# Loading the weights of a batched matmul two matrices at a time in 12 KB runs, with the x cast on ScalarE and products in 32-column tiles

## The chip, the cores and the metric

One core of a Trainium2 chip. The metric is device time in microseconds (us) of the whole program; the runs of one version lie within 0.05 to 0.26% of each other here (0.47% for one). Every kernel is compared with the kernel before on the same chip. Ratios are the mean time of one kernel's fast runs over that of the other's of the same rounds, so they aren't quite the ratio of the medians quoted beside them. The runs were made on several chips; the kernel before took 523.76 to 524.06 us in their rounds, so medians of different rounds compare to some 0.3 us. The 95% interval of a ratio is about 0.9 us wide to each side.

The engines in the profile are PE (TensorE; PEld is its weight load), DVE (VectorE), ACT (ScalarE), POOL (GpSimd) and SP (SyncE, which issues all transfers here). Data moves on 16 DMA engines. In this kernel every transfer has 128 rows and is moved as 128 packets, and for every 8 of them there is a 4-byte packet that reports completion: the kernel before has 24,832 of the first and 3,104 of the second.

## The reference

```python
b1, b2, m, k, n = 8, 16, 256, 512, 384
x      = randn(b1, b2, m, k)   # float32
weight = randn(b1, b2, k, n)   # float32
return np.matmul(x, weight).astype(np.float32)
```

128 independent products of 256 x 512 by 512 x 384: 67 MB of x and 101 MB of weights are read, 50 MB are written.

## The kernel before

It works in groups of four batches (the last four are cut into two pairs). A group's x is one transfer, each row of a batch matrix of weights is its own run, and the output is one transfer. Casts to bf16 are on VectorE, transposes of x and products on TensorE, and ScalarE copies the products out of PSUM.

```python
def load(e, a):                     # SyncE
    ...                             # x: 128 rows, 16 KB each, one transfer a group
    for i in range(G):              # weights: one matrix a transfer, 128 rows of 6 KB
        e.wait_ge(w_cast, a.m + (i + 1 - WS))
        e.dma_start(w_sb[...][:],
            w_rows[...].rearrange("(p ko) n -> p ko n", ko=KO)).then_inc(...)

def cast(e, a):                     # VectorE
    e.tensor_copy(out=x_bf[...], in_=x_sb[...]).then_inc(x_cast, 1)   # 128 x 4096
    cast_w(0)                                                         # 128 x 1536
    for q in range(G):                                                # transposes out of PSUM
        e.tensor_copy(out=xt[...], in_=pt[...]...).then_inc(t_copied, 1)
    for i in range(1, G):
        cast_w(i)

def copy_out(e, a):                 # ScalarE: 16 copies a group, 32 rows each
    for i in range(G):
        for g in range(G):
            e.copy(out=out_sb[...][i * C : (i + 1) * C, g : J * G : G, :],
                   in_=po[...][g * C : (g + 1) * C, :, :N])
```

SyncE issues the loads three groups ahead of the stores, all on one queue: first the loads of group n + 3, then the store of group n. A load waits until its buffer's last content has been cast.

## Time and profile before

| | kernel before |
|---|---|
| time | 524.05 us (first three runs), 523.94 with a fourth |
| span of the profiled run | 521.7 us |
| DMA | 218.16 MB in 27,940 packets, 9 tenths busy or more in 38 of 40 slices |
| busy share of PE, DVE, ACT | 62%, 52%, 78% |

A row of the slices cuts the span into 40 equal parts, and each digit is the busy share in tenths. Since the DMA row is full from end to end and no compute row is, the table is read as: the transfers set the time. The prediction below shows the lines.

### The profile page before, as it was taken

What the parts mean: (1) busy time and instruction counts of PE and PEld (TensorE: products, weight loads), DVE (VectorE), ACT (ScalarE), POOL (GpSimd) and SP (SyncE); (2) the same over time, 40 slices, a digit from 0 to 9 for tenths busy, and PEclk for the clock granted to TensorE, in tenths of its full rate; (3) what the DMA queues carried; (4) which work ended last, traced back from release to release, by engine and by line L of the source; (5) the groups of instructions that cost most, each with busy time, mean ns of one, the idle gap of its engine ahead of it and who ended that gap; (6) DMA issues with size and microseconds to landing.
All of it is one profiled execution on the core that took longest, in us unless ns stands there. A gap on an engine that the chain in (4) does not pass through costs nothing.

```text
span 521.7 us, 5583 instructions
## 1 busy us (share of the span) xinstructions
PE 323.8 (62%) x1536; PEld 192.3 (37%) x1536; DVE 270.0 (52%) x289; ACT 406.9 (78%) x511; POOL 0.7 (0%) x6
## 2 busy tenths in 40 slices
PE   1666565675767666675666856667566656666563
PEld 1433233442434333443334433243333434333341
DVE  2666546644466444566345663446644466444551
ACT  0699997697796879778977699777898786886972
POOL 0000000000000000000000000000000000000000
PEclk9999989667696687769677596787967896677976
DMA  8999999999999999999999999999999999999996
GB/s 330 424 422 423 421 427 423 424 423 423 426 431 424 422 421 426 428 429 421 420 427 427 428 424 421 423 427 429 427 422 421 425 429 428 422 423 423 426 427 258
DMA packets 27940, 218.16 MB, mean 418 GB/s; under 512 B 3104, under 2 KB 3104, under 8 KB 19744
## 3 DMA queue, kind: packets, MB, share of 16 engines
q1 hardware_dynamic: 27936, 218.12, 99.8%
q8 instruction: 1, 0.02, 0.0%
q14 instruction: 3, 0.02, 0.0%
HBM read 167.77 MB, written 50.33 MB: 418 GB/s over the span
## 4 chain that ended last, share of the span: by engine, by line
DMA 89%; DVE 7%; issue 1%; PE 1%; SPq 0%; DVEq 0%; ACTq 0%; ACT 0%
DMA x_sb<-in_x_dram 85%; DVE x_bf L158 7%; DMA w_sb<-in_weight_dram 4%; PE po L197 1%; SPq L121 0%; DVE x_t L167 0%; DVE w_bf L152 0%; DVEq L157 0%; ACTq _compat.py:109 0%; ACT out_sb L213 0%; SPq L304 0%; SPq L49 0%
## 5 line engine op out<-in xcount | busy, mean ns | idle before, releaser
L213 ACT COPY out_sb<-po 32x768 f32<-32x768 f32 (+1 forms) x504 | 397.9, 790 | 107.4 <-PE po L197 100.6
L197 PE MATMUL po<-w_bf,x_t 128*128 128x384 bf16 x1024 | 227.6, 380 | 139.9 <-ACT out_sb L213 103.6
L197 PEld LDWEIGHTS po<-w_bf,x_t 128*128 128x128 bf16 x1024 | 104.2, 109 | 254.7 <-ACT out_sb L213 126.9
L158 DVE CAST x_bf<-x_sb 128x4096 bf16<-128x4096 f32 (+1 forms) x33 | 73.6, 2229 | 215.6 <-DMA x_sb<-in_x_dram 215.6
L184 PE MATMUL pt<-identity,x_bf 128*128 128x128 f32 x512 | 96.9, 365 | 50.6 <-DVE x_bf L158 50.6
L152 DVE CAST w_bf<-w_sb 128x1536 bf16<-128x1536 f32 x128 | 117.5, 952 | 1.7 <-DMA w_sb<-in_weight_dram 1.5
L184 PEld LDWEIGHTS pt<-identity,x_bf 128*128 128x128 f32 x512 | 88.1, 218 | 67.0 <-issue 62.3
L167 DVE COPY x_t<-pt 128x1024 bf16<-128x1024 bf16 x128 | 84.4, 687 | 22.9 <-PE pt L184 22.3
L213 ACT ACT_TABLE_LOAD x7 | 9.0, 1283 | 1.6 <-ACTq L277 1.5
masks.py:199 POOL TENSOR_SCALAR_AFFINE_SELECT identity<-identity 128x128 f32<-128x128 f32 x1 | 0.3, 292 | 0.2 <-POOL identity L238 0.2
L238 POOL MEMSET identity<- 128x128 f32 x1 | 0.2, 204 | 0.5 <-SPq L49 0.5
L293 POOL MEMSET const-bfloat16-1.0<- 128x1 bf16 x1 | 0.1, 101 | 0.0
L293 POOL MEMSET const-uint8-127<- 128x1 uint8 x1 | 0.1, 101 | 0.0
L293 POOL MEMSET const-float32-0.0<- 128x1 f32 x1 | 0.1, 98 | 0.2 <-issue 0.2
L293 POOL MEMSET const-float32-1.0<- 128x1 f32 x1 | 0.1, 98 | 0.0
## 6 DMA issues: line engine op xcount, KB each, us to landing
w_sb<-in_weight_dram SPq DMA_DIRECT2D x128, 768.0 KB, 28.0
x_sb<-in_x_dram SPq DMA_DIRECT2D x31, 2048.0 KB, 29.6
out_dram<-out_sb SPq DMA_DIRECT2D x31, 1536.0 KB, 27.4
x_sb<-in_x_dram SPq DMA_DIRECT2D x2, 1024.0 KB, 24.3
out_dram<-out_sb SPq DMA_DIRECT2D x2, 768.0 KB, 8.4
```

The lines of the kernel that those rows point to most:

```text
L152: e.tensor_copy(out=w_bf[(a.m0 + i) % WBS][:], in_=w_sb[(a.m0 + i) % WS][:]).then_inc(w_cast, 1)
L158: e.tensor_copy(out=x_bf[a.slot(BS)][:, : J * G], in_=x_sb[a.slot(XS)][:, : J * G]).then_inc(x_cast, 1)
L167: e.tensor_copy(out=xt[:, j, :, :, g : g + 2].rearrange("k h i g c e -> k g (h i) (c e)"), in_=pt[(a.m0 + q) % PT][:].bitcast(bf16).rearrange(
L184: ins = e.transpose(pt[(a.m0 + q) % PT][:, rr, h, :], words[:, 2 * q + rr, h :: KO // 2], identity[:],)
L197: ins = e.matmul(po[(a.m0 + i) % PO][:, j, :N], xt[:, j, ko // 2, i, :, :, ko % 2].rearrange("k g c -> k (g c)"), w_bf[(a.m0 + i) % WBS][: ...
L213: ins = e.copy(out=out_sb[a.slot(OS)][i * C : (i + 1) * C, g : J * G : G, :], in_=po[(a.m0 + i) % PO][g * C : (g + 1) * C, :, :N],)
L238: e.memset(identity[:], 0.0).then_inc(id_done, 1)
L293: nc = _bacc.Bacc("TRN2", target_bir_lowering=False, num_devices=1)
```

## The change

The intent is fewer and longer contiguous runs in the weight loads. A row of two matrices is 12 KB only if a row holds eight consecutive rows of weights; the first matrix then lies in lanes 0 to 63, the second in 64 to 127, and each cast takes a half of the lanes to the half where it belongs. The contraction index is thereby permuted, so x must be permuted alike, which its cast does, now on ScalarE. And the products of the four batches share one PSUM tile, 32 rows each, so that one copy of 128 rows takes them out. Loads run four groups ahead, the last four batches are no longer cut into pairs, and the last group's store goes out in four pieces.

```diff
-            e.dma_start(
-                w_sb[(a.m0 + i) % WS][:],
-                w_rows[bass.ds(a.m * K + i * K, K)].rearrange("(p ko) n -> p ko n", ko=KO),
+        for d in range(G // D):                      # D = 2 matrices a load
+            e.dma_start(
+                w_sb[slot][:],
+                w_rows[bass.ds(n * (G * K) + d * (D * K), D * K)].rearrange(
+                    "(p k) n -> p k n", k=S * KO     # 8 rows, 12 KB
 ...
+            for a in range(D):                       # VectorE: half-lane casts
+                for h in range(S):
+                    e.tensor_copy(
+                        out=w_bf[...][h * HP : (h + 1) * HP],
+                        in_=w_sb[slot][a * HP : (a + 1) * HP, h * KO : (h + 1) * KO, :],
+                    ).then_inc(w_cast, 1)
 ...
-        e.tensor_copy(out=x_bf[...], in_=x_sb[...]).then_inc(x_cast, 1)
+        for h in range(S):                           # ScalarE, after two output copies
+            ins = e.copy(out=x_bf[...][:, :, h],
+                in_=x_sb[...].rearrange("p r (q s c) -> p r s q c", s=S, c=KO)[:, :, h])
 ...
+                    for i in range(G):               # TensorE: four tiles of 32 columns
+                        mine = slice(i * C, (i + 1) * C)
+                        ins = e.matmul(po[...][mine, rr, :N],
+                            x_t[...][:, 2 * q + rr, ko // 2, mine, ko % 2], w_bf[...][:, ko, :], ...)
 ...
-    LAG = 3
+    LAG = 4
```

## The prediction

> **What bounds the kernel now.** I read the page's slices first, then its DMA parts, the chain of work that ended last, the costliest groups, and last the timeline of one steady group and of the tail.
>
> ```profile
> ACT  0699997697796879778977699777898786886972
> DMA  8999999999999999999999999999999999999996
> GB/s 330 424 422 423 421 427 423 424 423 423 426 431 424 422 421 426 428 429 421 420 427 427 428 424 421 423 427 429 427 422 421 425 429 428 422 423 423 426 427 258
> DMA packets 27940, 218.16 MB, mean 418 GB/s; under 512 B 3104, under 2 KB 3104, under 8 KB 19744
> ...
> DMA 89%; DVE 7%; issue 1%; PE 1%; SPq 0%; DVEq 0%; ACTq 0%; ACT 0%
> ```
>
> The DMA row is at 9 in 38 of 40 slices and the rate is flat at 420 to 431 GB/s; only the first and the last slice are low. The chain is 89% DMA. So the kernel moves 218 MB through 16 full engines, and no compute engine sets its time. The ACT row is the highest compute row, but it has gaps everywhere, and the groups say what they are:
>
> ```profile
> L213 ACT COPY out_sb<-po 32x768 f32<-32x768 f32 (+1 forms) x504 | 397.9, 790 | 107.4 <-PE po L197 100.6
> ...
> L158 DVE CAST x_bf<-x_sb 128x4096 bf16<-128x4096 f32 (+1 forms) x33 | 73.6, 2229 | 215.6 <-DMA x_sb<-in_x_dram 215.6
> ...
> L152 DVE CAST w_bf<-w_sb 128x1536 bf16<-128x1536 f32 x128 | 117.5, 952 | 1.7 <-DMA w_sb<-in_weight_dram 1.5
> ...
> L167 DVE COPY x_t<-pt 128x1024 bf16<-128x1024 bf16 x128 | 84.4, 687 | 22.9 <-PE pt L184 22.3
> ```
>
> VectorE, the first consumer, waits 215.6 us for x. A steady group of four batches takes 16.13 us: the x casts of the timeline start at 255.99, 272.14 and 288.28.
>
> ```profile
> 255.99 2.29 DVE L158 CAST x_bf<-x_sb 128x4096 bf16<-128x4096 f32 x1 [7.70 <-DMA x_sb<-in_x_dram]
> 258.41 3.33 PE L184 MATMUL pt<-identity,x_bf 128*128 128x128 f32 x16 [1.88 <-DVE x_bf L158]
> 262.81 2.76 PE L197 MATMUL po<-w_bf,x_t 128*128 128x384 bf16 x16 [1.07 <-DVE x_t L167]
> 270.78 2.74 PE L197 MATMUL po<-w_bf,x_t 128*128 128x384 bf16 x8 [0.91 <-ACT out_sb L213]
> 272.14 2.29 DVE L158 CAST x_bf<-x_sb 128x4096 bf16<-128x4096 f32 x1 [6.97 <-DMA x_sb<-in_x_dram]
> ```
>
> The two product bursts give the pace of a 384-column matmul: less the 0.33 us of the last one's own duration, (2.76 - 0.33) / 15 = 162 ns with the clock free, and (2.74 - 0.49) / 7 = 321 ns with it halved.
>
> **What a packet costs** decides the gain, and the page doesn't show it, so I sorted the trace's packet records by size. There is one packet per contiguous run (16,640 of 6,144 B, 3,968 of 12,288 B, 3,968 of 16,384 B), so runs aren't cut. Shortest durations: 234, 460 and 611 ns, so 4,096 B more cost 151 ns (434 GB/s over 16 engines) and the rest is about 7 ns a packet whatever its size. Packets overlap a little, so durations overstate; I fitted 2 us windows between 50 and 480 us (16 engines times the window = sum of packets times cost) and got 235 ns for 6 KB, 458 for 12 KB and 609 for 16 KB. Check: a group has per engine 8 x 16 KB, 32 x 6 KB and 8 x 12 KB packets: 4.87 + 7.52 + 3.66 = 16.05 us, against 16.13 measured. Idle engine time, counted from the same records, is 0.3 us in all up to 507 us, and 2.8 us (averaged over 16 engines) after it: the tail.
>
> [...]
>
> **The change, part by part.**
>
> *Weight loads.* 16,384 packets of 6 KB become 8,192 of 12 KB: 8,192 x (2 x 235 - 458) / 16 = 6.1 us less of full DMA time. If reads of 12 KB come at 461 ns, their mean duration as writes now, it is 4.6 us. x (16 KB) and output (12 KB) runs stay. Completions fall from 3,104 to about 2,100 at 9 ns recorded each, 0.6 us at most; the fit gives them no cost, and I leave them out.
>
> *Half-lane casts.* Eight of 64 x 1536 a group in place of four of 128 x 1536. Time goes with elements per lane, so 8 x 0.95 = 7.6 us, plus 4 x 0.69 of copies: 10.4 us of VectorE a group where it was 2.29 + 3.8 + 2.76 = 8.85. Beside a 15.9 us DMA period: hidden.
>
> *x cast on ScalarE.* [...] The output copies fall from 16 of 32 rows to 4 of 128 rows, 4 x 0.79 = 3.2. [...] Hidden, and it gains nothing since ScalarE wasn't the bound.
>
> *Products in four tiles.* 128 matmuls of 32 weight columns and 384 moving in place of 32 full ones. If four run side by side there are 32 steps of 162 ns (321 throttled); allowing a third more for imperfect overlap, 7 us, or 10.3 throttled without that allowance. With transposes of at most 3.4 us and about 1 us of hand-over, PE needs 11 to 15 us of 15.9: hidden but closest to the edge.
>
> *The loop through ScalarE.* The next x cast now stands behind two output copies[...]. The x slot is freed about when this group's last weights land; its refill then has the store, x, weights and store before it in the queue, 3.7 + 4.9 + 7.3 + 3.7 = 19.6 us. So later frees open no gap.
>
> *The tail.* Before, it runs dry because the last groups' stores are issued late:
>
> ```profile
> 484.38 22.73 DMA w_sb<-in_weight_dram
> 507.13 0.45 DVE w_bf L152
> ...
> 509.34 4.96 PE po L197 x16
> 514.30 0.02 issue
> 514.33 0.79 ACT out_sb L213
> ```
>
> From 507 us there are 4.8 us of stores left for the queue but 9 us of work until the last store may start. In the new kernel the lag is four groups: when the last weights land, stores 27 to 30 (4 x 3.7 us) are still to be moved, 14.6 us. The last group needs 3.8 (four casts) + 0.7 + 7 to 10.3 + 0.8 = 12.3 to 15.6 us until its last quarter is copied, and its first three quarters' stores fill another 2.8. So the 2.8 us of idle tail should go nearly all; I take 2 to 2.8.
>
> *Sum.* 524.05 - 6.1 - 2.8 = 515.2 at best; 524.05 - 4.6 - 2 = 517.4 at the careful end. I choose 516.0, 1.5% less.
>
> **The rivals.**
>
> *Tiles don't run side by side.* Then 128 x 162 ns = 20.7 us of products a group, with transposes and hand-over 25, times 32: 800 us. Even two at a time (10.4 + 4.4 = 14.8) is hidden, so only near-complete serialization hurts. For it: PE loads weights before each matmul, four times as many. Against: [...]the sequencer passes four transposes with their weight loads between two register operations 115 ns apart in the trace, so issue isn't the limit. I give 7%.
>
> *VectorE becomes the bound.* [...]between 1,536 and 4,096 elements it now pays (2294 - 952) / 2560 = 0.524 ns an element; twice that adds 0.8 us a cast, 8 x 1.76 + 2.8 = 16.8 us a group plus hand-over, 32 x 17 = 545 us.[...] 3%.
>
> *The longer runs give nothing* (12 KB reads cost two of 6 KB): only the tail is left, 521 to 522 us. Against: 16 KB reads already show the low cost per byte. 6%.
>
> *More than counted:* completions (0.6 us)[...]; 513 us. 12%.
>
> **Range and chances.** DMA keeps setting the end in all but the first two rivals. The width around 516.0 comes from the packet cost (1.5 us), the tail (1 us), the run-to-run spread (0.9 us), and on the high side from the third rival: 513.3 to 520.5. Faster by over 2% needs 513.6 or less, which asks for the last rival: 0.12. Slower by over 2%: 0.10. Within 2%: 0.78.
>
> **What would show it.** Right: DMA still at 9 in all middle slices at about 429 GB/s instead of 424, a group every 15.9 us, 12,288 B reads at about 460 ns, almost no packets between 2 and 8 KB but the last stores' 512, [...]VectorE near 10.4 us a group, no empty stretch of the DMA before the last store. Wrong: DMA slices below 9 in the middle with PE or VectorE above 90%; VectorE casts above 1.1 us; a product quarter above 2.6 us; or 12 KB reads above 468 ns.

The cut marks stand for what was said of the hardware without a trace or run of this case to show it: ScalarE's time for the x cast, with the two sums built on it (ScalarE's load of a group, and the loop through ScalarE), the reasons why tiles and half-lane casts should behave as assumed, and a second reason for the last rival. That ScalarE's work and its loop are hidden, the third more for imperfect overlap of the tiles, and the 513 us of the last rival are estimates, shown by nothing at that point. The second rival is that a half-lane cast takes twice the time an element.

The other assumptions have these measured numbers. Clock free and halved: the granted clock was 1.00 and 0.50 in the two product bursts with 162 and 321 ns. Time by elements per lane: a VectorE cast took 952 ns for 1,536 elements, 1,227 for 2,048 and 2,294 for 4,096 on 128 lanes before, and 955 for 1,536 on 64 lanes after; a ScalarE copy of 768 elements took 789 ns on 32 lanes and 792 on 64 before, and 802 on 128 after.

## The result and the profile after

The changed kernel takes **520.08 us** (519.83 to 520.43, 4 runs) against 523.94 for the kernel before: ratio 0.9925, 95% interval 0.9908 to 0.9942. That is "within 2%", as called, but the gain is 3.9 us where 8 were predicted. That it lies inside the range is luck: its upper end was kept for the third rival (longer runs that give nothing), which didn't happen.

From the page of the changed kernel: its slices, packets and chain of work that ended last.

```profile
DVE  0878867655577555775556765557755577555670
ACT  3065462454234553245542445423454324553242
...
DMA  8999999999999999999999999999999999999995
GB/s 332 431 426 426 427 427 429 430 426 429 430 428 429 431 426 428 428 431 431 425 429 429 430 430 429 427 428 429 430 430 428 426 431 430 429 428 427 428 431 214
DMA packets 18868, 218.16 MB, mean 421 GB/s; under 512 B 2096, under 2 KB 2096, under 8 KB 2608
...
DMA 81%; DVE 12%; issue 2%; PE 2%; ACT 1%; SPq 0%; DVEq 0%; ACTq 0%
```

The DMA row is still full, the rate is up from about 424 to 429 GB/s, packets are down by a third, and ScalarE has emptied out, to 41% busy from 78%. The last slice is lower than before (214 against 258). The costliest groups, in the same columns as before (line, engine, operation, shapes, count, then busy us and mean ns, then idle time and releaser):

```profile
L148 DVE CAST w_bf<-w_sb 64x1536 bf16<-64x1536 f32 x256 | 244.5, 955 | 179.4 <-DMA w_sb<-in_weight_dram 166.7
L181 PE MATMUL po<-w_bf,x_t 128*32 128x384 bf16 x4096 | 231.4, 400 | 121.0 <-DVE x_t L154 121.0
L195 ACT COPY out_sb<-po 128x768 f32<-128x768 f32 x128 | 99.2, 802 | 290.2 <-PE po L181 290.2
...
L130 ACT CAST x_bf<-x_sb 128x2048 bf16<-128x2048 f32 x64 | 118.4, 1901 | 6.1 <-DMA x_sb<-in_x_dram 6.1
```

A half-lane cast takes 955 ns, as worked out; each of the two x casts of a group takes 1,901. Half-lane casts start 0.99 us apart ((7.86 - 0.955) / 7), where three full-lane casts in a row, 0.952 us each, started 0.87 apart before ((2.69 - 0.952) / 2); why wasn't looked for. VectorE waits 166.7 us for weights, so it isn't the bound. One steady group, from the timeline (start, us, engine, what):

```profile
428.41 3.70 ACT L130 CAST x_bf<-x_sb 128x2048 bf16<-128x2048 f32 x2
430.05 7.86 DVE L148 CAST w_bf<-w_sb 64x1536 bf16<-64x1536 f32 x8 [5.65 <-DMA w_sb<-in_weight_dram]
...
432.24 2.18 PE L167 MATMUL pt<-identity,x_bf 128*128 128x128 f32 x16 [1.98 <-ACT x_bf L130]
...
437.94 2.48 DVE L154 COPY x_t<-pt 128x1024 bf16<-128x1024 bf16 x4
...
438.69 8.11 PE L181 MATMUL po<-w_bf,x_t 128*32 128x384 bf16 x128 [4.27 <-DVE x_t L154]
```

The 128 tiles take 8.1 us here and 6.9 in the last group, where one after the other would need 20.7 (128 x 162 ns): they do run side by side. By the start times of the last group's records, four tiles start within 12 ns of each other, every 320 ns in its first part (granted clock 0.50) and every 163 ns in the rest (0.96). One full 128-column matmul took 321 and 162 ns before, at a granted clock of 0.50 and 1.00. So four tiles cost what one full matmul did, and the prediction's allowance of a third wasn't needed. On VectorE 7.86 us of casts and 2.48 of copies leave 5.65 us of waiting for weights in each period: that is its room.

**The tail, engine by engine.** The rows below are the DMA part of the page for the tail alone, 23 us in 40 slices; first before (from 499 us), then after (from 496 us).

```profile
DMA  9999999999999999999999998954202999100000
GB/s 385 420 431 399 395 445 381 467 381 431 438 438 449 459 459 385 417 470 449 406 385 513 385 395 374 427 246 192 85 32 85 438 395 438 54 21 0 0 0 0
```

```profile
DMA  9999999999999999999889989979211000000000
GB/s 427 470 406 406 406 492 406 427 385 492 427 427 406 449 449 406 406 449 449 369 347 433 401 347 379 369 289 417 102 75 43 27 21 27 27 5 0 0 0 0
```

Before, there is a dip and then a last burst; after, there is no dip, but a long low foot at about 27 GB/s. One of 16 engines at full speed moves 27 GB/s (12,288 B in some 458 ns). So the foot is one engine working alone. A mean over 16 engines hides this; the trace's completion records don't, since each transfer has 16 of them, taken as one an engine. Worked out from those records (us from the span's start; they don't name the engine, so "first" and "last" are by order of landing, and the quarters are told apart by one engine's regular step of 0.92 us):

```
store                       first engine   15th engine   last engine
before, group 30 (1.5 MB)     512.22         514.54        516.41
before, last pair (0.75 MB)   519.02         519.20        520.10
after,  group 30 (1.5 MB)     507.87         510.30        512.99
after,  last quarter          512.50         513.99        516.68
```

One engine is 4.2 us behind the first in the kernel before and 5.1 behind in the changed one. In the packet records its last packets follow each other without a break in both kernels. In the kernel before they start at 516.16, 516.39, 516.62, 516.85, 517.09, 517.32, 517.55, 517.78, 518.01 and so on, every 0.23 us to the end at 519.64, straight through the dip of the others.

### The profile page after: what moved, and what is told of

It is laid out like the page before. It is cut to its first block, busy times and chain, and to the rows that moved or that the text cites. A ratio compares the mean times of both kernels' runs of the same rounds, so it can differ in the third digit from the quotient of the medians.

```text
span 518.3 us, 11239 instructions
## 1 busy us (share of the span) xinstructions
PE 315.5 (61%) x4608; PEld 198.8 (38%) x4608; DVE 323.9 (62%) x384; ACT 212.7 (41%) x193; POOL 0.7 (0%) x6
## 2 busy tenths in 40 slices
DMA packets 18868, 218.16 MB, mean 421 GB/s; under 512 B 2096, under 2 KB 2096, under 8 KB 2608
## 4 chain that ended last, share of the span: by engine, by line
DMA 81%; DVE 12%; issue 2%; PE 2%; ACT 1%; SPq 0%; DVEq 0%; ACTq 0%
DMA w_sb<-in_weight_dram 81%; DVE w_bf L148 12%; PE po L181 2%; ACT x_bf L130 0%; DVEq _compat.py:109 0%; SPq L108 0%; ACT out_sb L195 0%; SPq L100 0%; DVE x_t L154 0%; DVEq L143 0%; DVEq L230 0%; SPq L107 0%; ACTq L194 0%; SPq L288 0%; SPq L54 0%
## 5 line engine op out<-in xcount | busy, mean ns | idle before, releaser
L148 DVE CAST w_bf<-w_sb 64x1536 bf16<-64x1536 f32 x256 | 244.5, 955 | 179.4 <-DMA w_sb<-in_weight_dram 166.7
L181 PE MATMUL po<-w_bf,x_t 128*32 128x384 bf16 x4096 | 231.4, 400 | 121.0 <-DVE x_t L154 121.0
L195 ACT COPY out_sb<-po 128x768 f32<-128x768 f32 x128 | 99.2, 802 | 290.2 <-PE po L181 290.2
L181 PEld LDWEIGHTS po<-w_bf,x_t 128*32 128x32 bf16 x4096 | 124.5, 117 | 225.4 <-DVE x_t L154 130.9
L167 PE MATMUL pt<-identity,x_bf 128*128 128x128 f32 x512 | 84.0, 329 | 73.0 <-ACT x_bf L130 73.0
L130 ACT CAST x_bf<-x_sb 128x2048 bf16<-128x2048 f32 x64 | 118.4, 1901 | 6.1 <-DMA x_sb<-in_x_dram 6.1
L167 PEld LDWEIGHTS pt<-identity,x_bf 128*128 128x128 f32 x512 | 74.3, 213 | 84.9 <-issue 84.9
L154 DVE COPY x_t<-pt 128x1024 bf16<-128x1024 bf16 x128 | 79.5, 683 | 1.0
```

Source lines behind the costliest of these rows:

```text
L130: ins = e.copy(out=x_bf[s % BS][:, :, h], in_=x_sb[s % XS][:].rearrange("p r (q s c) -> p r s q c", s=S, c=KO)[:, :, h],)
L148: e.tensor_copy(out=w_bf[(s * G + d * D + a) % WBS][h * HP : (h + 1) * HP], in_=w_sb[slot][a * HP : (a + 1) * HP, h * KO : (h + 1) * KO, : ...
L154: e.tensor_copy(out=x_t[s % TS][:, 2 * q : 2 * q + 2], in_=pt[(s * T + q) % PT][:].bitcast(bf16),).then_inc(t_copied, 1)
L167: ins = e.transpose(pt[(s * T + q) % PT][:, rr, h, :], words[:, 2 * q + rr, h :: KO // 2], identity[:],)
L181: ins = e.matmul(po[(s * T + q) % PO][mine, rr, :N], x_t[s % TS][:, 2 * q + rr, ko // 2, mine, ko % 2], w_bf[(s * G + i) % WBS][:, ko, :], ...
L195: e.copy(out=out_sb[s % OS][:, 2 * q : 2 * q + 2, :], in_=po[(s * T + q) % PO][:, :, :N],).then_inc(o_copied, 1)
```

## The experiments

All results below are correct unless said otherwise. "Theory A" in the expectations is that one slow DMA engine, which never pauses, sets the end; "rival D" is that the last group's work sets it.

### The weight run length alone

The changed kernel with a gap in the middle of each destination row, which cuts each 12 KB run into two of 6 KB and leaves all else.

```diff
-    w_sb = sbuf("w_sb", [P, S * KO, N], fp32, WS)
+    w_sb = sbuf("w_sb", [P, S, KO * N + 16], fp32, WS)
-                w_sb[slot][:],  ... "(p k) n -> p k n", k=S * KO
+                w_sb[slot][:, :, : KO * N],  ... "(p s k) n -> p s (k n)", s=S, k=KO
```

> The changed kernel, with its weight loads cut into runs of 6,144 B again by a gap in the middle of each destination row; loads, completions, casts and products stay. Theory A (the run length on the slowest DMA engine is the whole gain): 16,384 packets cost 233.2 - 4 = 229 to 233 ns each in place of 8,192 of 458, so 8,192 x 8 ns / 16 = 4.1 us slower than the changed kernel, 524.0 to 524.5 us. Rival B (half as many completions bring the gain): within 1 us of the changed kernel, 520 to 521. Rival C (6.1 us of stream gain as predicted, given back elsewhere): 526.

Measured: 522.70 us (ratio to before 0.9979). The page confirms the edit: the completions (under 512 B) stay, the packets under 8 KB are back.

```profile
DMA packets 27060, 218.16 MB, mean 419 GB/s; under 512 B 2096, under 2 KB 2096, under 8 KB 18992
```

The run length is worth 522.70 - 520.08 = 2.6 us. That is less than theory A's 4.1 and not the rivals' 0 or 6, so run length is the larger part of the gain, but not all. By the completion records of the store of group 30, the first engine is 3.0 us later than in the changed kernel (510.87 against 507.87), but the slowest is 4.6 us behind it in place of 5.1.

### Run length and number of loads

The same 6 KB runs, but each load cut into two loads, so that weight runs and completions are both those of the kernel before.

```diff
+            for h in range(S):
+                half = slice(h * KO, (h + 1) * KO)
+                e.dma_start(w_sb[slot][:, half], rows[:, half]).then_inc(w_in[slot], 16)
```

> The changed kernel with each 12 KB load issued as two loads of 6 KB runs, so that weight runs and completions are those of the kernel before; casts, products and stores stay as changed. If the gain is only runs and completions: 1,024 completions more at 6 ns / 16 = 0.4 us over the run with 6 KB runs alone, 523.1 us; if all that the change brought is in the way weights are loaded: 523.7 to 524.2, as the kernel before. A time well below 523 would mean that the new compute part brings some of the gain.

Measured: 524.07 us, ratio 1.0001 (0.9984 to 1.0017), the kernel before to a hair. Everything else of the change is still in it: half-lane casts, x cast on ScalarE, tiles, single output copies, the lag of four, the store in pieces. So together these bring nothing (which doesn't say that each one brings nothing), and the whole 3.9 us come from the weight loads: 2.6 from longer runs and 524.07 - 522.70 = 1.4 from half as many loads. The two runs were on different chips; by their differences to the kernel before it is 1.3.

### The transfers alone

The changed kernel's transfers in the same order and buffers, with no work on any compute engine: a load waits for the landing of the load before in its slot, and zeros are stored. All four give a wrong result. They differ only in how weights are loaded.

```diff
-            e.wait_ge(x_cast, n + (1 - XS))
+            e.wait_ge(x_in[s % XS], (t * (U // XS) + s // XS) * 16)
-                e.wait_ge(w_cast, ...)
+                e.wait_ge(w_in[slot], (t * (U * G // D // WS) + s * G // D // WS) * 16)
 ... (all compute removed, GpSimd sets the zeros; 6 KB in two-matrix loads: the gap as above; 24 KB: D = S = 4; one matrix a load: D = S = 1)
```

> The changed kernel's transfers alone, in the same order and with the same buffers, each load waiting for the landing of the load before in its slot; no casts, products or output copies, zeros are stored (a wrong result on purpose). Theory A (the DMA stream of the slowest engine is all that counts): within 1 us of the changed kernel less its last receipt, 518.5 to 520.3 us. If work on the engines costs something in the tail or the middle: clearly below 518.

> The transfers alone with weight runs of 6 KB and as many completions as the changed kernel (a wrong result on purpose). Theory A: 4.1 us more than the transfers alone with 12 KB runs. The prediction's fit (2 x 235 - 458 = 12 ns a pair): 6.1 us more.

> The transfers alone with weights as the kernel before loads them, one matrix of 6 KB runs a load, 128 loads (a wrong result on purpose). Completions: 0.4 us over the transfers alone with 6 KB runs and 64 loads, 521.6 us; if smaller loads cost more than their completions: 522 or more.

> The transfers alone with weight runs of 24 KB, four matrices a load (a wrong result on purpose). If a packet costs about 7 ns beside its bytes: 4,096 packets fewer, 4,096 x 7 / 16 = 1.8 us less than with 12 KB runs, and 1,024 completions fewer at 6 ns / 16 = 0.2 us: 2 us less.

| weights | loads | time | median packet | mean packet |
|---|---|---|---|---|
| 6 KB runs, one matrix a load | 128 | 522.36 us | 236 ns | 237.1 ns |
| 6 KB runs, two matrices a load | 64 | 521.24 us | 234 ns | 236.3 ns |
| 12 KB runs | 64 | 518.03 us | 460 ns | 462.1 ns (with the stores) |
| 24 KB runs | 32 | 515.54 us | 912 ns | 915.2 ns |

Run length is worth 3.2 us, below the 4.1 and 6.1 expected, and the number of loads 1.1, about the split seen with compute (2.6 and 1.4). These two differences are about as large as an interval of a ratio; that the runs with and without compute agree, and the packets below, carries them. The transfers alone take 518.03 us, 0.5 less than the 518.5 to 520.3 of theory A and 2.1 less than the changed kernel, so work on the engines does cost something; "Where the x cast runs" below looks for it. The packets explain the sizes. On one engine, a packet starts 3 to 4 ns before the one before it ends, so its cost is taken as its duration less 4. Two 6 KB packets cost 2 x 232.3 = 464.6, one of 12 KB 458.1, and 8,192 x 6.5 / 16 = 3.3 us. With one matrix a load, 6 KB packets are 0.8 ns longer on average, 16,384 x 0.8 / 16 = 0.8 us, and 1,024 more completions at 6 ns each are 0.4 us: 1.2 against 1.1 measured. The reason for the 0.8 ns wasn't looked for. Going to 24 KB brought the transfers alone another 2.5 us; with compute it wasn't built, since it needs quarter-lane casts. An estimate, if each takes as long as a half-lane cast: 16 x 0.955 = 15.3 us of VectorE a group beside 2.7 us of copies, more than the DMA's period of 15.9.

### Is there idle time in the tail to win?

First, the last store as one transfer of 12 KB runs after the last copy, in place of four pieces.

```diff
-            store(e, 0, NG, n, T if n == NG - 1 else 1)
+            store(e, 0, NG, n)
```

> The changed kernel with the last group's output stored in one transfer of 12 KB runs after its last quarter is copied (510.3 us in the profile), in place of four transfers of 3 KB runs from 506.2 us on. Theory A (the end is set by one slow DMA engine that is never idle; it is still busy with the store before until about 512.5 us): no slower, 519.8 to 520.2 us. Rival D (the tail is bound by the last group's work, with the DMA waiting for it): 2 to 3 us slower, 522 to 523.

Measured: 519.54 us (ratio 0.9917). Waiting with the whole store for the last quarter cost nothing. That it is even 0.5 us faster isn't the store's doing: the store of group 30, which the edit doesn't touch, had already landed on the slowest engine at 512.47 in place of 512.99, and from there to the last landing it is 3.6 us here and 3.7 in the changed kernel.

Then the last group was made late on purpose, by needless copies on ScalarE before its first output copy.

```diff
+        if isinstance(n, int) and n == NG - 1 and q == 0:
+            for j in range(3):                       # 8 in the second run
+                if j:
+                    e.wait_ge(pace, j)
+                e.copy(out=scr[:], in_=x_sb[s % XS][:, :2]).then_inc(pace, 1)
```

> The changed kernel with about 3.3 us of needless copies on ScalarE ahead of the first output copy of the last group, so that its last store is issued that much later. Theory A: the slow DMA engine gets to the last quarter's store at about 515.3 us, and it could start from 511.7 on, so there are 3.6 us of slack: no change, 520.0 to 520.5 us. Rival D: 3.3 us slower, 523.4.

> The same with about 8.8 us of needless copies. Theory A: 8.8 less the 3.6 us of slack, 5.2 us slower, about 525.3 us. Rival D: 8.8 us slower, about 529.

The timelines of the two, three lines each: the needless copies, the issue of the four pieces, the last output copy.

```profile
505.27 3.20 ACT L201 COPY scr<-x_sb 128x1024 f32<-128x1024 f32 x3 [8.24 <-PE po L183]
...
509.19 4.11 SPq L123 DMA_DIRECT2D out_dram<-out_sb  x4
...
512.14 0.80 ACT L202 COPY out_sb<-po 128x768 f32<-128x768 f32 x1 [0.50 <-PE po L183]
```

```profile
505.14 8.58 ACT L201 COPY scr<-x_sb 128x1024 f32<-128x1024 f32 x8 [8.72 <-PE po L183]
...
514.44 6.63 SPq L123 DMA_DIRECT2D out_dram<-out_sb  x4
...
519.92 0.80 ACT L202 COPY out_sb<-po 128x768 f32<-128x768 f32 x1 [1.76 <-PE po L183]
```

Measured: 520.06 us with 3.2 us of copies (ratio 0.9928; 0.9925 without them) and 525.87 with 8.6 (ratio 1.0035). The last copy ended at 510.33 without delay, at 512.94 and at 520.72. So 2.6 us of delay are free, and of 10.4 us of delay 5.8 show, 4.6 are swallowed. The last group's work isn't on the path that sets the end; the slow engine's queue of stores is.

Last, the lag.

```diff
-    LAG = 4
+    LAG = 3
```

> The changed kernel with three groups loaded ahead of the stores, as before, in place of four. When the last weights land, three stores (28 to 30, 11 us) are left instead of four. Theory A: the slow engine is through with them 4 + 11 us after the others' last weights, about 512.5 us, as it has moved store 27 earlier instead; the total is the same and the last quarter still has its slack: 519.8 to 520.5 us. Prediction (the lag of four closes an idle tail of 2 to 2.8 us): 522 to 523.

Measured: 520.09 us (ratio 0.9923), the same. The fourth group of lag, which the prediction credited with closing the tail, does nothing.

### Sparing an engine

If one engine is late, give it less. The store of group 30 was cut into 120 and 8 rows.

```diff
+            lanes = [slice(0, P)]
+            if isinstance(n, int) and n == NG - 2:
+                lanes = [slice(0, 120), slice(120, P)]
```

> The changed kernel with the last store but one (group 30) issued as 120 rows, which go to 15 DMA engines, and 8 rows, which go to 8 of them, so that one engine has 3.7 us less to do at the end. Theory A, if the slow engine is the one left out: the end falls to the next slowest (1.7 us behind it) plus 0.5 us for a ninth row: 1.0 to 1.6 us faster, 518.6 to 519.1. If the slow engine is another: 0 to 0.5 us slower. Rival D (no slow engine sets the end): no gain.

Measured: 523.13 us, unsteady (521.36 to 523.81). The store's 23 completion packets (2,103 in all for 2,096) fit 15 and 8 engines, as meant. This failed, and not as either theory had it: in that stretch 47 of the 12 KB packets took 571 to 1,696 ns in place of 460. With the uneven split packets slowed by more than it spared; why wasn't looked for, and which engine is the slow one this run doesn't tell.

### Where the x cast runs

The x cast back on VectorE, in the same permuted form.

```diff
     def prepare(e, t, U, s):
+        cast_x(e, t, U, s)              # and no longer in ScalarE's step
 ...
-            ins = e.copy(
+            ins = e.tensor_copy(
                 out=x_bf[s % BS][:, :, h],
```

> The changed kernel with the x cast back on VectorE, ahead of the weight casts of its group, permuted as before in two instructions. VectorE then has 10.4 + 2 x 1.2 = 12.8 us of 15.9 a group, ScalarE 3.2. Theory A (engines are hidden behind the DMA): 520.0 to 520.5 us. If the cast on ScalarE matters: over 1 us off.

Measured: 518.81 us (ratio 0.9901), 1.3 us faster than the changed kernel, which theory A didn't expect. Its page:

```profile
DVE  2999987877788777887778787778877788777880
```

VectorE is fuller, 77% busy, and still not the bound: it waits 95.5 us for x and weights. The completion records show where the 1.3 us lie. For the load of x of group 30:

```
kernel                 first engine   median   last engine
changed                  470.07       470.62     474.20
x cast on VectorE        470.01       470.67     472.86
transfers alone          470.22       470.60     472.45
```

First and median are the same within 0.2 us; the last engine is 1.3 us less late. This supports most directly that the slowest engine sets the end: 15 engines nearly unchanged, one better by 1.34 us, and the time better by 1.27. The same records show when the lag arises. How far the last engine (in brackets the 15th) is behind the first, in us, at four loads of x:

```
kernel                 group 6       group 14      group 22      group 30
before                 2.23 (1.87)   2.31 (2.21)   3.10 (2.32)   3.91 (2.32)
changed                2.40 (1.89)   2.69 (2.39)   3.40 (2.41)   4.13 (2.39)
x cast on VectorE      2.00 (1.87)   2.11 (2.07)   2.47 (2.12)   2.85 (2.23)
transfers alone        1.48 (1.16)   1.90 (1.74)   2.11 (1.88)   2.23 (2.13)
```

In the first two kernels one engine alone falls back, by some 0.07 us a group; with the cast on VectorE by about half of that. The kernel before has its x cast on VectorE too, so the place of the cast can't be the whole cause.

Two runs asked why that engine is less late. The first adds two needless casts a group on ScalarE to that version, the second delays the issue of each x load to the last weight cast of the group before in its slot.

```diff
+                    for h in range(S):               # first run, ScalarE, after two output copies
+                        e.copy(out=junk[:, :, h], in_=idle[...]...[:, :, h])
```

```diff
-            e.wait_ge(x_cast, n + (1 - XS))          # second run
+            e.wait_ge(w_cast, n * (G * S) + (G * S - XS * G * S))
```

> The kernel with the x cast on VectorE, plus two needless casts of the same size and pattern on ScalarE in each group, at the place of the ScalarE cast, from a buffer that nothing waits for. If ScalarE's busy time or its reads slow the slowest DMA engine: back to 520 us. If the moment at which the x slot comes free does it: 518.8, as without them.

> The kernel with the x cast on VectorE, but each x load waits for the last weight cast of the group before in its slot, so that it is issued some 10 us later, later than with the cast on ScalarE. If the moment of issue slows the slowest DMA engine: 520 us or above. If ScalarE's work does: 518.8, as without the wait.

Measured: 518.86 us (ratio 0.9908) and 518.40 us (ratio 0.9899). Neither ScalarE's work nor the later issue brings the lag back (2.75 and 2.43 us at the load of group 30), so both explanations fall. What slows the one engine, in the kernel before and when ScalarE does the real cast, stays open.

### A version that beats both

The x cast on VectorE and the last store in one transfer.

> The kernel with the x cast on VectorE and the last store in one transfer. Both were faster alone, by 1.3 and 0.5 us; if they add up, 518.2 to 518.5 us, below both kernels.

Measured: 518.78 us (ratio 0.9903, 0.9886 to 0.9919). It beats both kernels, by 1.0% the one before, but the two gains don't add up: it equals the x cast on VectorE alone, as it should if the 0.5 us of the one-piece store were a difference in the slow engine's lag.

## Why the prediction was right or wrong

**Right: the bound and the verdict.** The DMA stayed full, the engines stayed hidden, and the time moved by less than 2%. The loads of VectorE and TensorE came out as worked out: a group has 10.2 us of VectorE where 10.4 were said, and the products take 6.9 to 8.1 us where 7 to 10.3 were said. ScalarE has 6.8 us, with 1.90 for each of the two x casts. The period is 15.89 us on the first engine, from landings of x 24 groups apart, where 15.9 was said. The first two rivals (tiles one after the other, VectorE as the bound) didn't happen. The third, longer runs that give nothing, is refuted by the run with 6 KB runs: 2.6 us slower.

**Wrong: the tail term, 2 to 2.8 us, was zero.** The step that failed is "From 507 us there are 4.8 us of stores left for the queue but 9 us of work until the last store may start", and the idle 2.8 us under it. That figure was a mean over 16 engines. It was read as a queue that ran dry; for most engines it did, but one was 4.2 us behind and never paused, and the end waits for the last. The 4.8 us were misread too: the store packets in flight or still to start at 507 us, without the last pair's, come to 8.1 us of 16 engines. A hint stood in the prediction's own check: 16.05 us a group by the packets against 16.13 by VectorE's x casts. Those wait for the last engine, whose landings are 16.10 us apart where the first engine's are 16.03. Removing idle time of the other 15 is worth nothing, in the changed kernel too: the one-piece store, the 3.2 us of needless work and the lag of three all leave the time where it was or below. The sentence in "What would show it", no empty stretch before the last store, came true and meant nothing.

**Mis-sized: the weight loads, 4.6 to 6.1 us, brought 3.9.** Longer runs do cost less, as said, but by less: two packets of 6 KB cost 2 x 233.2 = 466.4 ns, one of 12 KB 458.4. The term that was off is "8,192 x (2 x 235 - 458) / 16 = 6.1". The fit of costs to 2 us windows had the right sum and the wrong split: it gave 6 KB packets 235 ns where duration less the 4 ns overlap gives 237.2 - 4 = 233.2 in that same trace (its 458 and 609 for the longer ones agree with 457.4 and 608.2), and the completions nothing. With 233.2, and 458.4 for the 12 KB packets of the changed kernel, the term is 8,192 x 8.0 / 16 = 4.1 us. The completions do cost: the next packet starts 6 ns after the start of one, so 1,024 fewer are 0.4 us. 4.5 us is then the stream's gain, and the first engine's period agrees: (16.03 - 15.89) x 32 = 4.5.

**Lost on the way: about 0.6 us.** The slowest engine, not the first, counts, and it is 5.1 us behind in the changed kernel where it was 4.2 behind. Four runs with the same steady loop (the one-piece store, both runs of needless copies, the lag of three), with one profile each, have 4.3 to 4.7, so part of this differs from program to program. Moving the x cast to VectorE alone brings it to 3.7 and gains 1.3 us. Why is open.

**The rival "more than counted"** had most of the completions' share right (0.4 of its 0.6 us), but that is within the 4.5 us, not on top of 6.1. The rest of its 513 us wasn't shown.

## What to carry to other kernels

In a stream like this one, with 16 DMA engines full, the slowest of them set the end: count idle time on that one, from completion records per engine, before crediting anything to a tail that looks idle in the mean. The cost of a packet is best read from start to next start on one engine; a fit over windows can be right in sum and wrong by half in a difference. And prove what a large rewrite's parts are worth by undoing the smallest one that could explain the gain: here one changed destination layout and one split load took all of it back.
